# A hybrid encoder block: the first queries of group A plain behind v, returned sums as one fp32 value, a bank for each product, and queries and keys loaded over 128 partitions

## The chip, the cores and the metric

The kernel runs on one core of one Trainium2 chip. A core has five engines with instruction streams of their own: TensorE (PE) for matmuls into PSUM banks, VectorE (DVE), ScalarE (ACT) and GpSimd (POOL) for elementwise work, and SyncE (SP), which here issues nearly all transfers between DRAM and SBUF. Each engine runs its instructions in program order and waits on semaphores of the others. The metric is the device time of one execution in microseconds.

## The reference

One layer on 1024 frames of width 1024, in fp32. Eight heads (group A) attend within chunks with a learned bias, eight (group B) use stick-breaking attention; head pairs are computed together. Cut to what matters:

```
h    = rmsnorm(x, norm1_g)
proj = h @ w_in                       # q, k, v of group A, then of group B
qa, ka, va, qb, kb, vb = split(proj)
ya = chunked_attention(qa, ka, va, rel_bias)      # 64-frame chunks, 9-chunk key band, softmax
yb = stick_breaking_attention(qb, kb, vb)         # causal, 128-query blocks
mixed = concat([rmsnorm(ya, norm_a_g), rmsnorm(yb, norm_b_g)])
x = x + mixed @ w_out
x = x + conv_gated_mlp(rmsnorm(x, norm2_g), ...)  # up-projection, depthwise conv, SiLU gate, down-projection
return rmsnorm(x, final_g)
```

## The kernel before

**Precision.** Every fp32 operand of a projection is kept as two parts: a high part, rounded to the matmul type, and the low rest. A product is then three matmuls, high by high, high by low, low by high. A split is thus a copy (ScalarE or GpSimd) and a subtraction (the helper at L125, on VectorE unless said otherwise).

**Stages.** The first is the v projection by Strassen's scheme with seven products of four steps each (`steps`, in the order 1, 2, 5, 6, 7, 3, 4); between its steps a hook `extra(n)` issues work of other engines by hand. `t1` and `t2`, sums of blocks of the input's transpose, are used again later: `keep` (L367) stores their high and low parts to DRAM while v is computed, `bring_back` (L372) loads them at step (4,0), eight transfers of 512 KB, ahead of the stores of v's results by `give` (L399, and L401 for one-row stores of 2 KB each).

Then `early(n)` for n = 0 to 3 projects queries and keys of the head pairs of group B, each by seven products (`product`, L1180, twelve matmuls of 512 columns) in the order a, e, b, a, c, e, c. a and e are the two halves of one PSUM tile of two banks (`eqk`), b and c tiles of one bank. After product a, ScalarE copies a to b (L1213); after product b it copies b to c (L1234). `early_out` (L1190) scales a result, splits it and stores both parts to DRAM. `Pieces` holds the sums and splits of a pair's weights (`whole`, `make`, `split`), made one group ahead.

Then the two sweeps: four groups of group B (scores L909 and L910, scan on VectorE L918, sigmoid on ScalarE L927, transposes L945, output L959) and four of group A (scores L1009 and L1010). The text calls the head pairs B0 to B3 and A4 to A7. Between the sweeps' blocks `filler` matmuls are laid: `project_qk(n)` for n = 4 to 7 (queries and keys of group A, 48 matmuls each) and the output projection. A planner hands out filler at a rate per block (`RATE_B`, `RATES_A`) with a lead (`LEAD_B`, `LEAD_A`). `load_qk(n)` (L809) brings a pair's queries and keys: six SBUF tiles `qa, qb, ka, kb, la, lb` of 128 partitions, each filled by two transfers of 64 partitions (256 KB), high parts from `qh_d` and `kh_d`, low ones from `ql_d` and `kl_d`. The tiles are double: those of pair n+2 use the slots of pair n. Behind the sweeps come the output projection, the up- and down-projections of the channel mixer and the last norm.

Of the kernel before, what the change touches and what calls it, by code (L numbers as in the profile page):

```python
# [16 lines left out]
P = 128  # L17
T = 1024
# [39 lines left out]
def r32(ap):  # L58
    return ap.bitcast(F32)
# [3 lines left out]
def tile_hybrid_block(  # L63
# [128 lines left out]
    with tc.tile_pool(name="kp", bufs=2) as kp:  # L192
# [48 lines left out]
        def all_v():  # L241
# [104 lines left out]
                    if src is not None:  # L346
                        split(h, l, src)

            first, second = (big(f"v_x{i}") for i in range(2))
            X = area(first, second)  # L350
            steps = [(p, k) for p in (1, 2, 5, 6, 7, 3, 4) for k in range(4)]

            def staged(name):
# [2 lines left out]
                    for j in range(4)  # L356
                ]

            kept = {0: (t_high[0], t_low), 1: (t_high[1], t2_low)}
            again = {}  # L360

            def keep(n, k):
                for t, r in zip(kept[n], halves):
                    nc.sync.dma_start(t_d[n][k][:, r], r32(t[k]))

            def bring_back():
                for n in range(2):  # L367
                    for k in range(4):
                        t = slot(4 + k, f"t1_{k}", F32R) if n == 0 else kp.tile(
                            [P, T], F32R, tag=f"y{k}", name=f"t2_{k}", bufs=1  # L370
                        )
                        nc.sync.dma_start(r32(t), t_d[n][k])  # L372
                        again[n, k] = t[:, lo], t[:, hi]

            c11, u2, m5 = [], [t[:, lo] for t in xin[:4]], [t[:, hi] for t in xin[:4]]

# [26 lines left out]
            def extra(n):  # L403

                i = n - ROW_STEP
                if 0 <= i < 16:
                    S.activation(row[i % 2], row[i % 2], AF.Square, accum_out=ms[:, i : i + 1])
                    if i < 14:
                        bring_row(i + 2)
                if steps[n] == (7, 2):  # L410
                    for j in range(4):
                        S.copy(m5[j], X[j])
                    raws[0] = [wp.tile([P, D], F32, tag="wr", name="raw0_q", bufs=1)]
                    nc.sync.dma_start(raws[0][0], w_in[12])
                if steps[n] in ((5, 1), (5, 3)):
                    for k in range(n - 9, n - 7) if n == 9 else range(2, 4):
                        keep(0, k)
                if n in (12, 14):
                    for k in (0, 1) if n == 12 else (2, 3):
                        keep(1, k)  # L420
                if steps[n] == (3, 0):
                    bring_raw(0, 10)
# [12 lines left out]
                if steps[n] == (4, 1):  # L435
                    give(m5, 1, 1)
                    give(u2, 0, 1)
                if steps[n] == (4, 2):
                    ahead[0].make("s1")
                    ahead[0].split("s1")  # L440
                    ahead[0].make("s2")
                if steps[n] == (4, 3):
                    give(staged("c21"), 1, 0, Y)
                    ahead[0].split("s2")
                    bring_raw(1, 0)
                    bring_raw(2, 1)
                    bring_raw(2, 2)
                    bring_raw(3, 3)

            def t1(k):  # L450
                a = xin[k]
# [5 lines left out]
            def begin(n):  # L457
# [19 lines left out]
                if n == 7:  # L477
# [5 lines left out]
                            sums(6, k)  # L483
                    parts(6, 0)

            begin(-1)
            for n, (p, k) in enumerate(steps):
                bank = X if p in (1, 2, 5, 3) else Y
# [20 lines left out]
                "t1": [again[0, k] for k in range(4)],  # L509
                "t2": [again[1, k] for k in range(4)],  # L510
                "t3": list(zip(t_high[0], t_low)),
                "t4": list(zip(t_high[1], t4_low)),
            }

        t_d = [
            [dp.tile([P, T], F32, tag=f"t{n}{k}", name=f"t_d{n}_{k}") for k in range(4)]
            for n in range(2)
        ]
        qk_d = [
            {w: dp.tile([P, T], F32, tag=f"{w}{n}", name=f"{w}_d{n}") for w in ("qh", "ql", "kh", "kl")}  # L520
            for n in range(8)
        ]
        raws, ahead = {}, []

        def bring_raw(n, x):

# [181 lines left out]
        w_list = []  # L708
        for n in range(4, 8):
            ct = n - 4  # L710
            w_list += [(w_in[ct], f"q{n}"), (w_in[ct + 4], f"k{n}")]
# [63 lines left out]
        def spill_qk(n, what, outs, g):  # L775

            t, r = {}, rows(g)

            def high():
                t["h"] = kp.tile([P, GW], F32R, tag="tmp", name=f"{what}{n}_h{g}", bufs=3)  # L780
                (S.copy if what == "q" else GP.tensor_copy)(t["h"], t["f"])

            def keep(part, x):
                return load(256, lambda: nc.sync.dma_start(qk_d[n][f"{what}{part}"][:, r], r32(t[x])))

            head, kept = fs.pair(
                on_v(GW, lambda: scaled(outs[g], g, 0.125 if what == "q" else 1.0, f"{what}{n}", t)),
                on_s(GW, high) if what == "q" else on_g(230, high),
                keep("h", "h"),
                [on_v(GW, lambda: sub(t["f"].bitcast(F32R), t["f"], t["h"]), "VL"), keep("l", "f")],  # L790
            )
            qk_kept[n] += kept
            return head

        def load_qk(n):

            s = 6 * (n % 2)
            names = ("qa", "qb", "ka", "kb", "la", "lb")
            ts = [slot(s + i, f"{x}{n}", F32R) for i, x in enumerate(names)]
            qk_of[n] = ts  # L800
            qa, qb, ka, kb, la, lb = ts
            d = qk_d[n]
            moves = (
                ((qa, A, "qh", A), (qa, B, "ql", A), (ka, A, "kh", A), (ka, B, "kh", A), (la, A, "kl", A), (la, B, "kl", A)),
                ((qb, B, "qh", B), (qb, A, "ql", B), (kb, B, "kh", B), (kb, A, "kh", B), (lb, B, "kl", B), (lb, A, "kl", B)),
            )

            def bring(t, x, w, y):
                nc.sync.dma_start(r32(t[x, :]), d[w][y, :])  # L809

            qk_chains[n] = [
                flow.add(*(load(256, lambda m=m: bring(*m)) for m in ms), after=qk_kept[n]) for ms in moves
            ]

        def advance():

            n = len(qk_of)
            if n < 8 and at["qk"] >= n - 2 and (n < 4 or len(qk_kept[n]) == 8):
# [367 lines left out]
        def early_out(n, what, src, r, f=None):  # L1186

            if f is None:
                f = kp.tile([P, GW], F32, tag="tmp", name=f"e{what}{n}f", bufs=3)
            V.scalar_tensor_tensor(  # L1190
                out=f, in0=src, scalar=0.125 if what == "q" else 1.0, in1=rb1[:, r],
                op0=ALU.mult, op1=ALU.mult,
            )
            h = kp.tile([P, GW], F32R, tag="tmp", name=f"e{what}{n}h", bufs=3)
            S.copy(h, f)
            sub(f.bitcast(F32R), f, h)
            nc.sync.dma_start(qk_d[n][f"{what}h"][:, r], r32(h))
            nc.sync.dma_start(qk_d[n][f"{what}l"][:, r], f)

        def early(n):  # L1200

# [11 lines left out]
            S.copy(b, a)  # L1213
            if n == 0:
                ob = big("rb1_ob")
                across(ob[:, lo], rn1, 0, 4)
                across(ob[:, hi], rn1, 4, 8)
                S.copy(rb1, ob)
                for what in ("s4", "s3"):
                    own.make(what)  # L1220
                    own.split(what)
            own.split("a22")
            if n == 1:
                bring_raw(3, 10)
            if nxt:
                nxt.whole()
# [1100 lines left out]
```

## Time and profile before

| | us |
|---|---|
| median of three runs (1241.77 to 1245.99) | 1243.87 |
| profiled execution | 1245.49 |
| its span, first to last instruction | 1243.8 |
| TensorE busy in it | 1199.5 (96%) |
| v projection ends, early(0) begins | 86.5 |
| early(1) begins | 124.2 |
| early(3) ends, first filler of the sweep | 190.55 |
| first score product of the B sweep | 196.67 |
| first score product of the A sweep | 362.2 |
| first score product of pair A7 | 483.80 |

A busy row gives, for each engine, busy time, share of the span and number of instructions. Where the profile names a wait it gives the engine and line that waited, what released it, the total, the number of waits and the longest. In a table of stretches each engine has its busy time and, in brackets, its instructions; the last three columns are the granted clock, the mean busy share of the sixteen DMA engines and the GB/s that they moved.

### The profile page before, as it was taken

The page shows a single profiled execution, that of the slowest core. Times are in us where ns is not written, and L with a number is a line of the kernel's source. Part 1 is how long each engine was busy: PE and PEld are TensorE (multiplying, and loading weights), DVE is VectorE, ACT ScalarE, POOL GpSimd, SP SyncE. Part 2 cuts the span into 40 slices and gives each one's busy share as a digit, 9 for nine tenths or more (in the row PEclk, how much of TensorE's full clock was granted, in tenths as well). Part 3 has the DMA queues.
Part 4 walks back from the last instruction along what each step waited for, and adds up shares of the span by engine and source line. Part 5 has one row for each costly group of instructions (what it writes and reads, how often), then busy time and mean ns, then how long its engine had stood idle before and what let it go on. Part 6 is the DMA issues. An engine that isn't in the chain of part 4 may idle for free.

```text
span 1243.8 us, 17412 instructions
## 1 busy us (share of the span) xinstructions
PE 1199.5 (96%) x6428; PEld 992.8 (80%) x6428; DVE 944.2 (76%) x1443; ACT 688.3 (55%) x1225; POOL 153.2 (12%) x158
## 2 busy tenths in 40 slices
PE   9996898999999999989999999999999999999997
PEld 6774776888888788878878888888888888888887
DVE  7953645889857688747998776776777769969896
ACT  7772433666657677633576455555555555444424
POOL 0000012011121131044000000000000022041126
PEclk9997999999999999999999999999999999999999
DMA  8667339766865873123222212223222087330003
GB/s 291 220 202 271 119 127 269 184 177 160 211 181 165 232 220 95 52 88 124 76 102 85 96 67 92 85 68 102 76 77 102 34 325 318 128 144 1 1 1 136
DMA packets 74803, 171.14 MB, mean 138 GB/s; under 512 B 7767, under 2 KB 23255, under 8 KB 74718
## 3 DMA queue, kind: packets, MB, share of 16 engines
q1 hardware_dynamic: 74574, 169.92, 43.0%
q8 instruction: 51, 0.84, 0.3%
q14 instruction: 34, 0.28, 0.1%
q10 hardware_dynamic: 144, 0.11, 0.0%
HBM read 120.70 MB, written 49.30 MB: 137 GB/s over the span
## 4 chain that ended last, share of the span: by engine, by line
PE 66%; DVE 8%; DMA 6%; ACT 3%; issue 3%; POOL 1%; SPq 0%; DVEq 0%; ACTq 0%; POOLq 0%
PE u_a L1742 9%; PE u_c L1742 8%; PE u_e L1742 8%; PE dz L2241 8%; PE u_b L1742 4%; PE dj L2241 4%; PE dm L2241 4%; PE q_p L147 2%; PE tpb L945 2%; PE k_p L147 2%; PE yb L959 2%; PE pa L147 2%; PE dnl L2162 1%; DMA lb<-kl_d 1%; PE yy L1074 1%
## 5 line engine op out<-in xcount | busy, mean ns | idle before, releaser
L918 DVE TENSOR_TENSOR_SCAN acts<-zb,first 128x128 f32<-128x128 f32 (+7 forms) x64 | 86.4, 1351 | 15.6 <-ACT zb L927 15.6
L1766 DVE SCALAR_TENSOR_TENSOR vt<-cv,cst,vt 128x1023 f32<-128x1023 f32 (+1 forms) x44 | 58.2, 1323 | 3.3 <-ACT vt L1760 2.5
L1766 DVE SCALAR_TENSOR_TENSOR gt<-cg,cst,gt 128x1023 f32<-128x1023 f32 (+1 forms) x44 | 56.3, 1280 | 1.1 <-ACT gt L1760 0.3
L1040 ACT ACTIVATE pa<-sa,sta 128x640 f32<-128x640 f32 (+4 forms) x64 | 42.5, 665 | 18.8 <-DVE sta L1026 17.6
L927 ACT ACTIVATE zb<-zb 128x128 f32<-128x128 f32 (+7 forms) x64 | 40.9, 641 | 21.0 <-PE zb L910 19.7
L125 POOL TENSOR_TENSOR dx_0wl<-dr,dx_0wh 128x512 fp32r<-128x512 f32 x1 | 1.4, 1371 | 412.3 <-ACT dx_0wh L2008 412.3
L1760 ACT ACTIVATE gt<-cg,cst 128x1024 f32<-128x1024 f32 x22 | 27.4, 1245 | 36.9 <-DVE cg L1634 36.8
L949 ACT COPY tb<-tpb 128x128 f32<-128x128 f32 (+3 forms) x96 | 43.1, 484 | 6.4 <-PE tpb L945 5.6
L1065 ACT COPY pta<-tpa 128x512 f32<-128x512 f32 (+3 forms) x80 | 36.1, 479 | 14.6 <-PE tpa L1061 14.2
L945 PE MATMUL tpb<-ident,acts 128*128 128x128 f32 x288 | 43.2, 277 | 0.0
L1026 DVE TENSOR_REDUCE sta<-sa 128x1 f32<-128x640 f32 (+4 forms) x64 | 41.7, 654 | 1.2
L1061 PE MATMUL tpa<-ident,pa 128*128 128x128 f32 x240 | 38.3, 279 | 4.1 <-DVE sa L1022 3.1
L125 POOL TENSOR_TENSOR q_l<-q_r,q_h 128x256 fp32r<-128x256 f32 x16 | 13.3, 862 | 232.9 <-ACT q_h L740 208.9
L1631 DVE TENSOR_TENSOR up_r<-up_r 128x512 f32<-128x512 f32 x60 | 41.2, 687 | 0.8
L945 PEld LDWEIGHTS tpb<-ident,acts 128*128 128x128 f32 x288 | 33.3, 140 | 6.2 <-issue 2.6
L1061 PEld LDWEIGHTS tpa<-ident,pa 128*128 128x128 f32 x240 | 27.2, 140 | 13.1 <-ACT pta L1065 6.2
L1929 ACT COPY u_b<-u_a 128x512 f32<-128x512 f32 x19 | 10.8, 571 | 38.1 <-PE u_a L1742 38.1
L1023 DVE TENSOR_TENSOR sa<-sa,bias 128x256 f32<-128x256 f32 (+1 forms) x64 | 26.2, 413 | 6.0 <-PE sa L1010 4.8
L1074 PE MATMUL yy<-pta,v 128*64 128x128 f32 x480 | 30.0, 276 | 0.0
L959 PE MATMUL yb<-tb,dv 128*64 128x128 f32 x448 | 29.5, 273 | 0.0
L125 POOL TENSOR_TENSOR wo_l<-wo_r,wo_h 128x256 fp32r<-128x256 f32 x28 | 20.1, 745 | 70.1 <-ACT wo_h L740 70.1
L1074 PEld LDWEIGHTS yy<-pta,v 128*64 128x64 f32 x480 | 26.1, 137 | 3.3 <-issue 1.1
(1409 smaller groups left out, 4051.1 us busy)
## 6 DMA issues: line engine op xcount, KB each, us to landing
up_r<-in_w_up_dram SPq DMA_DIRECT2D x44, 512.0 KB, 3.6
act<-vt SPq DMA_DIRECT2D x22, 512.0 KB, 2.6
dr<-in_w_dn_dram SPq DMA_DIRECT2D x20, 512.0 KB, 7.0
dr<-act SPq DMA_DIRECT2D x20, 512.0 KB, 10.1
wv<-in_w_v_dram SPq DMA_DIRECT2D x16, 256.0 KB, 5.4
xin<-in_xT_dram SPq DMA_DIRECT2D x16, 256.0 KB, 5.4
row<-in_x_rows_dram SPq DMA_DIRECT2D x16, 256.0 KB, 3.2
t<-t_d SPq DMA_DIRECT2D x8, 512.0 KB, 7.7
```

Of the source, the lines that this page charges most:

```text
L147: PE.matmul(o, w[:, sl], t[:, rows(g)], start=first and i == 0, stop=last and i == 2,)
L918: V.tensor_tensor_scan(out=a[:, :w], data0=z, data1=first[:, :w], initial=1.0, op0=ALU.mult, op1=ALU.max,)
L945: PE.transpose(tp[:, cols(b)], self.a[h][:, cols(b0 + b)], ident)
L949: mine.append(flow.add(on_s(m * P, lambda o=o, tp=tp: S.copy(o, tp))))
L959: PE.matmul(yy[HS[h], :], (d if j else v)[:, off : off + 64], self.at[h][:, self.c0[h] + j * P : self.c0[h] + (j + 1) * P], start=j == 0, ...
L1026: V.tensor_reduce(out=st[:, 0:1], in_=full, axis=AX.XY if nk == 5 else AX.X, op=ALU.max, negate=True,)
L1040: on_s(w + 170, lambda: S.activation(po, full, AF.Exp, bias=st[:, 0:1], accum_out=st[:, 1:2])),
L1061: PE.transpose(tp[:, cols(b)], self.pr[src][:, cols(c)], ident)
L1074: PE.matmul(yy[HS[h], :], v[:, (i + c) * P + h * 64 : (i + c) * P + (h + 1) * 64], self.pt[:, 4 * h + c if c < 4 else 8 + h, :], start=c = ...
L1742: PE.matmul(o, w[:, cols(k)], t, start=start and k == 0 and i == 0, stop=k == 3 and i == 2, skip_group_check=True,)
L1766: V.scalar_tensor_tensor(out=t[:, : T - lag], in0=o[:, lag:], scalar=c1(c + ct), in1=t[:, : T - lag], op0=ALU.mult, op1=ALU.add,)
L2241: PE.matmul(o[m], w[:, cols(m)], t, start=i in (0, 1, 4, 5) and p == ps_[0] and j == 0, stop=p == ps_[-1] and j == 2, skip_group_check=True,)
```

## The change

It has five parts.

1. `first_query()`, called between v and early(0), computes the queries of pair 4 by the plain product (48 matmuls), with its own banks `q4_0` and `q4_1`. Their weight is loaded at step (7,2) and split at (4,0). `project_qk(4)` in the filler computes only the keys. The spreading of the norm's factor (`rb1`), `whole`, `s2`, `s4` and `s3` of the first pair move into it.
2. t1 and t2 are stored as one fp32 half each (2 MB in all in place of 4), come back behind the stores of v at step (4,2), and are split again by `split_again`: eight copies and eight subtractions.
3. The two-bank tiles of the v projection and of early(n) become tiles of one bank each (`zbank`).
4. Queries and keys are kept as `q_d[n]` and `k_d[n]` of shape `[2, P, T]` (high and low part), and a tile of 128 partitions is filled by one transfer of 512 KB: a query tile from both parts of a head, a key tile from one part, broadcast to both halves. 96 transfers become 48.
5. The rates and leads of the filler are smaller.

The core of the diff:

```diff
-RATE_B, LEAD_B = 10.0, 4.0
-RATES_A, LEAD_A = (11.0, 13.0, 13.0, 13.0), 6.5
+RATE_B, LEAD_B = 8.0, 4.0
+RATES_A, LEAD_A = (10.0, 10.0, 10.0, 10.0), 4.0
...
-            first, second = (big(f"v_x{i}") for i in range(2))
-            X = area(first, second)
+            X = [zbank(f"v_x{i}") for i in range(4)]
...
+            def keep(k):
+                nc.sync.dma_start(t_d[k], xin[k][:, hi])
+
+            def bring_back(k):
+                t = slot(k, f"t2_{k}", F32R) if k > 3 else kp.tile(
+                    [P, T], F32R, tag=f"y{k}", name=f"t1_{k}", bufs=1
+                )
+                nc.sync.dma_start(r32(t[:, hi]), t_d[k])
+                again.append(t)
+
+            def split_again(t):
+                S.copy(t[:, lo], r32(t[:, hi]))
+                sub(t[:, hi], r32(t[:, hi]), t[:, lo])
...
-                    bring_back()
-                    bring_raw(1, 11)
-                    ahead.append(Pieces(0))
-                    ahead[0].whole()
+                    lead["h"], lead["l"] = [
+                        wp.tile([P, D], F32R, tag=t, name=f"q4_{t}") for t in ("wh", "wl")
+                    ]
+                    S.copy(lead["h"], lead["r"])
+                    for r in halves:
+                        sub(lead["l"][:, r], lead["r"][:, r], lead["h"][:, r], GP)
...
                 if steps[n] == (4, 2):
+                    for k in range(KT):
+                        bring_back(k)
+                    ahead.append(Pieces(0))
                     ahead[0].make("s1")
                     ahead[0].split("s1")
-                    ahead[0].make("s2")
...
+        q_d = [dp.tile([2, P, T], F32, tag=f"q{n}", name=f"q_d{n}") for n in range(8)]
+        k_d = [dp.tile([2, P, T], F32, tag=f"k{n}", name=f"k_d{n}") for n in range(8)]
...
-            moves = (
-                ((qa, A, "qh", A), (qa, B, "ql", A), (ka, A, "kh", A), (ka, B, "kh", A), (la, A, "kl", A), (la, B, "kl", A)),
-                ((qb, B, "qh", B), (qb, A, "ql", B), (kb, B, "kh", B), (kb, A, "kh", B), (lb, B, "kl", B), (lb, A, "kl", B)),
-            )
...
+            def twice(part, h):
+                return k_d[n][part][None, h, :].to_broadcast([2, 64, T])
+
+            moves = [
+                [(q, q_d[n][:, h, :]), (k, twice(0, h)), (l, twice(1, h))]
+                for h, q, k, l in ((A, qa, ka, la), (B, qb, kb, lb))
+            ]
...
         def project_qk(n):
-            for what in ("q", "k"):
+            for what in ("q", "k") if n > 4 else ("k",):
...
-            z = big(f"eqk{n}")
-            a, e = z[:, lo], z[:, hi]
+            a, e = zbank(f"ea{n}"), zbank(f"ee{n}")
...
+        def first_query():
+
+            outs = [zbank(f"q4_{g}") for g in range(G)]
+            own = ahead[0]
+            for g in range(G):
+                for k in range(KT):
+                    mm3(outs[g : g + 1], lead["h"], lead["l"], cols(k), hh[k], hl[k], k == 0, k == KT - 1, (g,))
+                    if (g, k) == (0, 3):
+                        for i in range(2):
+                            ob = zbank(f"rb1_ob{i}")
+                            across(ob, rn1, 4 * i, 4 * i + 4)
+                            S.copy(rb1[:, rows(i)], ob)
+                    flow.work(0.68)
+                if not g:
+                    own.whole()
+                    own.make("s2")
+                    own.split("s2")
+                    again_all[0]()
+                    early_out(4, "q", outs[0], lo)
+                else:
+                    own.make("s4")
+                    own.split("s4")
+                    own.make("s3")
+                    own.split("s3")
+                    early_out(4, "q", outs[1], hi)
+
+        first_query()
```

What this makes of the order is seen at three places. The first is SyncE's queue behind early(2), where the loads of pair B0 begin. `qa` to `lb` are the SBUF tiles, the names behind the arrow the DRAM tiles, and the shape is the tile's in SBUF. Before:

```order
L809 DMA qa_1414<-qh_d_137 64x1024
L809 DMA qb_1415<-qh_d_137 64x1024
L809 DMA qa_1414<-ql_d_138 64x1024
L1197 DMA qh_d_149<-eq3h 128x512
L1198 DMA ql_d_150<-eq3f 128x512
L809 DMA qb_1415<-ql_d_138 64x1024
L809 DMA ka_1416<-kh_d_139 64x1024
L1197 DMA kh_d_151<-ek3h 128x512
L1198 DMA kl_d_152<-em_1359 128x512
L809 DMA kb_1417<-kh_d_139 64x1024
L809 DMA ka_1416<-kh_d_139 64x1024
```

and now:

```order
L803 DMA qa_1485<-q_d_137 128x1x1024
L803 DMA qb_1486<-q_d_137 128x1x1024
L1198 DMA q_d_140<-eq3h 128x512
L1199 DMA q_d_140<-eq3f 128x512
L803 DMA ka_1487<-k_d_145 128x1x1024
L1198 DMA k_d_148<-ek3h 128x512
L1199 DMA k_d_148<-em_1430 128x512
L803 DMA kb_1488<-k_d_145 128x1x1024
L1198 DMA q_d_140<-eq3h 128x512
L1199 DMA q_d_140<-eu_1431 128x512
L803 DMA la_1489<-k_d_145 128x1x1024
L803 DMA lb_1490<-k_d_145 128x1x1024
```

The twelve loads of 64 rows have become six of 128, all of them issued before the last stores of early(3)'s keys; the stores of early(3)'s queries stand behind two loads in place of three.

The second place is SyncE's queue at the end of the v projection, where t1 and t2 come back (`t`) and v is stored (`v_d`). Before:

```order
L372 DMA t_1_802<-t_d_1_134 128x1024
L372 DMA t_2_804<-t_d_2_135 128x1024
L372 DMA t_3_806<-t_d_3_136 128x1024
L529 DMA raw_11_808<-in_w_in_dram 128x1024
L399 DMA v_d_112<-xin_170 128x512
L399 DMA v_d_112<-xin_171 128x512
L399 DMA v_d_112<-xin_172 128x512
L399 DMA v_d_112<-xin_173 128x512
L399 DMA v_d_111<-xin_170 128x512
```

and now:

```order
L398 DMA v_d_111<-xin_157 128x512
L400 DMA v_d_111<-xin_157 1x512
L367 DMA t_0_821<-t_d_129 128x512
L367 DMA t_1_823<-t_d_130 128x512
L367 DMA t_2_825<-t_d_131 128x512
L367 DMA t_3_827<-t_d_132 128x512
L367 DMA t_4_829<-t_d_133 128x512
L367 DMA t_5_831<-t_d_134 128x512
L367 DMA t_6_833<-t_d_135 128x512
L367 DMA t_7_835<-t_d_136 128x512
L398 DMA v_d_112<-c_853 128x512
L398 DMA v_d_112<-c_854 128x512
```

The returns of t1 and t2 have moved behind eight stores of v and the four one-row stores, and are 512 columns wide in place of 1024.

The third is VectorE's queue around early(0). `raw` are the first pair's weights, `s_0` their sums, `t_0` to `t_7` the returned t1 and t2, `eq4f` and `eq0f` results read from PSUM banks (line 1190 before, 1191 now). Before, behind the root of the norm:

```order
L125 TENSOR_TENSOR qk0wl<-raw_q,qk0wh 128x1024
L228 TENSOR_TENSOR raw_10_705<-raw_10_705 128x512
L125 TENSOR_TENSOR s_0_859<-raw_10_705,s_0_859 128x512
L225 TENSOR_TENSOR raw_q<-raw_10_705,raw_q 128x512
L125 TENSOR_TENSOR s_0_887<-raw_q,s_0_887 128x512
L225 TENSOR_TENSOR raw_q<-raw_q 128x512
L125 TENSOR_TENSOR s_0_930<-raw_q,s_0_930 128x512
L225 TENSOR_TENSOR raw_q<-raw_q,raw_10_705 128x512
L125 TENSOR_TENSOR s_0_934<-raw_q,s_0_934 128x512
```

and now, ahead of the second bank of q4:

```order
L125 TENSOR_TENSOR qk0wl<-raw_11_683,qk0wh 128x1024
L225 TENSOR_TENSOR raw_11_683<-raw_10_685,raw_11_683 128x512
L125 TENSOR_TENSOR s_0_919<-raw_11_683,s_0_919 128x512
L125 TENSOR_TENSOR t_0_821<-t_0_821 128x512
L125 TENSOR_TENSOR t_1_823<-t_1_823 128x512
L125 TENSOR_TENSOR t_2_825<-t_2_825 128x512
L125 TENSOR_TENSOR t_3_827<-t_3_827 128x512
L125 TENSOR_TENSOR t_4_829<-t_4_829 128x512
L125 TENSOR_TENSOR t_5_831<-t_5_831 128x512
L125 TENSOR_TENSOR t_6_833<-t_6_833 128x512
L125 TENSOR_TENSOR t_7_835<-t_7_835 128x512
L1191 SCALAR_TENSOR_TENSOR eq4f<-q_0_874,rb_873 128x512
```

Eight subtractions for the returned sums stand between the first pair's `s2` and the reading of q4's first bank, a reading that was not there before; the operations of `s4` and `s3` stand behind it.

More of the change, by code (lines that the diff above doesn't have):

```diff
@@ L357, in staged @@
                 ]
[L359 to L370, printed above, removed]
-                        )
-                        nc.sync.dma_start(r32(t), t_d[n][k])
-                        again[n, k] = t[:, lo], t[:, hi]
+            again = []
+            def keep(k):
[9 more added lines that the diff above has]
+                sub(t[:, hi], r32(t[:, hi]), t[:, lo])
             c11, u2, m5 = [], [t[:, lo] for t in xin[:4]], [t[:, hi] for t in xin[:4]]
@@ L412, in extra @@
                         S.copy(m5[j], X[j])
[L413 to L420, printed above, removed]
+                    lead["r"] = wp.tile([P, D], F32, tag="wr", name="q4_r", bufs=1)
+                    nc.sync.dma_start(lead["r"], w_in[0])
+                for k in {5: (0, 1), 6: (2, 3), 7: (4, 5), 8: (6,), 9: (7,)}.get(n, ()):
+                    keep(k)
                 if steps[n] == (3, 0):
+                    bring_raw(0, 11)
                     bring_raw(0, 10)
@@ L484, in begin @@
                     parts(6, 0)
+            again_all.append(lambda: [split_again(t) for t in again])
             begin(-1)
@@ L513, in all_v, with kept_at @@
             }
[L515 to L523, printed above, removed]
+        t_d = [dp.tile([P, GW], F32, tag=f"t{k}", name=f"t_d{k}") for k in range(KT)]
+        q_d = [dp.tile([2, P, T], F32, tag=f"q{n}", name=f"q_d{n}") for n in range(8)]
+        k_d = [dp.tile([2, P, T], F32, tag=f"k{n}", name=f"k_d{n}") for n in range(8)]
+        raws, ahead, lead, again_all = {}, [], {}, []
+        def kept_at(n, what, part):
+            return {"q": q_d, "k": k_d}[what][n][part]
         def bring_raw(n, x):
@@ L783, in keep @@
             def keep(part, x):
-                return load(256, lambda: nc.sync.dma_start(qk_d[n][f"{what}{part}"][:, r], r32(t[x])))
+                return load(256, lambda: nc.sync.dma_start(kept_at(n, what, part)[:, r], r32(t[x])))
             head, kept = fs.pair(
@@ L1213, in early @@
             S.copy(b, a)
[L1214 to L1221, printed above, removed]
             own.split("a22")
             if n == 1:
+                bring_raw(3, 11)
                 bring_raw(3, 10)
```

29 lines of the change are left out of this document (13 added, 16 removed).

## The prediction

> **What bounds the kernel now.** I read the page first, then TensorE's waits up to the start of the B sweep, then the busy time by stretches, and last the transfers that the change reshapes. The page:
>
> ```profile
> span 1243.8 us, 17412 instructions
> PE 1199.5 (96%) x6428; PEld 992.8 (80%) x6428; DVE 944.2 (76%) x1443; ACT 688.3 (55%) x1225; POOL 153.2 (12%) x158
> PEclk9997999999999999999999999999999999999999
> DMA  8667339766865873123222212223222087330003
> GB/s 291 220 202 271 119 127 269 184 177 160 211 181 165 232 220 95 52 88 124 76 102 85 96 67 92 85 68 102 76 77 102 34 325 318 128 144 1 1 1 136
> DMA packets 74803, 171.14 MB, mean 138 GB/s; under 512 B 7767, under 2 KB 23255, under 8 KB 74718
> ```
>
> TensorE is busy 96% of the span, so a saving has to remove TensorE idle time or slow-clock time; the only slow slice of the clock row is the fourth, 93 to 124 us. Transfers keep the engines 0.5 to 0.8 busy while the sweeps run (slices 6 to 15), so the sweeps stay on TensorE only as long as their loads arrive. The profiled execution took 1245.49 us, 1.7 more than its span and 1.6 above the median 1243.87; the sum below is made against 1245.49.
>
> TensorE's waits between 86 and 240 us (total, number, longest):
>
> ```profile
> PE ec L1180 <- ACT ec L1234: 6.8, 1, 6.8
> PE eqk L1180 <- ACT eb L1213: 6.7, 4, 2.7
> PE zb L909 <- DVE acts L918: 3.2, 1, 3.2
> PE eb L1180 <- DMA t<-t_d: 1.8, 4, 0.7
> PE eqk L1180 <- ACT em L1230: 1.8, 1, 1.8
> ```
>
> and its timeline where early(3) ends and the sweep begins:
>
> ```profile
> 190.55 0.39 PE L147 MATMUL q_p<-hTh,q_h 128*128 128x512 f32 x1
> ...
> 196.67 0.28 PE L909 MATMUL zb<-ka,qa 128*128 128x256 f32 x1
> 200.08 0.35 PE L910 MATMUL zb<-la,qa 128*128 128x256 f32 x1 [3.13 <-DMA la<-kl_d]
> ```
>
> Between the first two stand 27 matmuls of q4: 6.12 / 27 = 0.227 us each at full clock. And the first score product already waits 3.13 us for a key load.
>
> **The change, part by part.**
>
> *The front: q4 plain behind v, fewer stored sums, a bank for each product.* The stretches of early(0), of early(1) to early(3), and of the sweep's start:
>
> ```profile
> 86.40:124.20 37.80, 26.70 (x94) 19.36 (x93) 15.20 (x23) 12.72 (x22) 0.00 (x0) 0.82 0.81 289
> 124.20:190.60 66.40, 60.45 (x254) 48.35 (x253) 36.94 (x53) 24.71 (x41) 8.41 (x11) 0.97 0.40 131
> 190.60:200.00 9.40, 6.35 (x29) 5.02 (x27) 2.68 (x4) 2.00 (x3) 0.00 (x0) 1.00 1.02 271
> ```
>
> An early group is 84 matmuls, 84 x 0.227 = 19.1 us. early(0) takes 37.8, so 18.7 are waits, slow clock and one microsecond of transposes that move elsewhere. The other three take 66.4 for 57.2, 9.2 over. The 6.8 us wait follows from the 4 MB of t1 and t2 coming back ahead of v's own stores on SyncE; now 2 MB come back, behind those stores. The four L1213 waits are product e waiting for a copy that reads the other half of its two-bank tile; with banks of their own they go, and the first e and a then wait for VectorE to read q4's banks. What stands in front of that reading on VectorE counts; the nearest rows on the chain of work are:
>
> ```profile
> 159.40 0.63 ACT eq2h L1195
> 160.05 0.70 DVE eq2f L125
> ```
>
> Ahead of the first bank's reading stand the eight new subtractions, 8 x 0.70 = 5.6 us, which cannot begin before t1 and t2 are back; ahead of the second one four more operations of `s4` and `s3` (2.8) beside the split of the first half (1.4). Over them lie q4's matmuls (48 x 0.227 = 10.9) and product a (2.7), if t1 and t2 come back in time. I bound the new waits by nothing and by 7 us (the subtractions wholly uncovered, and the split behind them) and take 5, since t1 and t2 now come back late. Gain: early(0) 18.7 - 1 - 5 = about 12; early(1) to (3) about 8; the sweep's start some 7, its 3.1 of load wait and the 3.2 for `acts` right behind it, both of which follow from early(3) ending late against the loads. Together 27; with the new waits at nothing 32, and with them at 7 and the sweep's start unchanged 18. At early(3)'s end the gain less what moved in is 12 + 8 - 10.9 - 1 = 8 us. The 48 matmuls of q4 only move: 10.9 us leave the sweeps and enter the front.
>
> *Less filler in the B sweep.* Of the 225 filler matmuls within the four B groups 186 remain, 39 x 0.227 = 8.9 us less to lay beside the scan on VectorE, which the rows of the sweep below show busy 28 to 35 of 40 us. Where VectorE is late nothing covers it: cost between 0 and 8.9, I take 4. The rates and leads only shift filler between groups; no row prices them, and the 4 holds for them too.
>
> *The loads of queries and keys.* 96 loads of 64 rows become 48 of 128. The number of bytes is the same (25.2 MB), and 48 issues on SyncE of some 0.6 us go, beside which TensorE works anyway. What changes is how a load can be cut up. The source of the new loads is `q_d[n][:, h, :]` or a key tile broadcast to `[2, 64, T]`: outermost a count of **2**, one of them with stride zero, then 64 rows of 4 KB. Before, both sides had 64 rows outermost. What the trace says of this are the seven smallest stores:
>
> ```profile
> L401 SPq DMA_DIRECT2D v_d<-xin x4: 235/236/236, 97.2 to 102.7; - x4
> L401 SPq DMA_DIRECT2D v_d<-c x2: 294/320/347, 80.5 to 81.3; - x2
> L401 SPq DMA_DIRECT2D v_d<-v_c x1: 304/304/304, 82.1 to 82.1; - x1
> ```
>
> They are single rows of 2 KB. The kernel issues 491 transfers (490 on SyncE, one on ScalarE; the view of DMA issues). If each ended with one small packet on each of 16 engines, and with the 16 rows of 128 bytes of the constants, there would be 491 x 16 + 16 = 7872 packets under 512 B. The page counts 7767, short by 105 = 7 x 15: exactly the seven stores whose outer count is 1 went over one engine, and every transfer with an outer count of 16 or more over sixteen. So the engines follow the shape. An outer count of 2 does not occur before. I take it that it gives 2 engines: no transfer of this kernel is seen cut inside its outermost count (a row of 2 KB stayed whole), and the stride between the two halves of the new source keeps them from being read as one run of 128 rows. The other reading is that the 4 KB rows inside are counted (128, so 16 engines).
>
> [...]
>
> The price, from the stretches of the sweep and the densest one of the run (last two columns: DMA share, GB/s):
>
> ```profile
> 168.00:200.00 32.00, 26.22 (x107) 20.82 (x105) 11.68 (x16) 9.65 (x15) 8.41 (x11) 0.95 0.71 203
> 200.00:240.00 40.00, 36.13 (x272) 30.41 (x273) 30.93 (x40) 22.51 (x46) 3.76 (x4) 0.96 0.86 210
> 240.00:280.00 40.00, 39.78 (x336) 33.94 (x336) 32.64 (x40) 27.15 (x52) 4.49 (x6) 1.00 0.72 191
> 280.00:320.00 40.00, 40.00 (x352) 34.56 (x349) 34.89 (x43) 26.62 (x55) 6.39 (x6) 1.00 0.70 178
> 320.00:360.00 40.00, 39.91 (x319) 33.75 (x318) 28.49 (x40) 25.01 (x49) 6.85 (x9) 1.00 0.59 170
> 360.00:400.00 40.00, 38.23 (x291) 32.40 (x291) 28.99 (x74) 29.59 (x61) 8.77 (x13) 1.00 0.69 183
> 400.00:440.00 40.00, 38.42 (x285) 32.18 (x281) 26.91 (x73) 28.45 (x67) 5.25 (x8) 1.00 0.84 248
> 440.00:480.00 40.00, 39.64 (x305) 33.53 (x304) 35.01 (x85) 28.65 (x66) 9.16 (x13) 1.00 0.65 175
> ...
> 1020.00:1030.00 10.00, 10.00 (x46) 8.24 (x44) 9.54 (x12) 4.67 (x8) 1.84 (x2) 1.00 1.03 410
> ```
>
> One busy engine moves 410 / (16 x 1.03) = 24.9 GB/s in the densest stretch, 170 / (16 x 0.59) = 18.0 in the thinnest. Half of a 524,288-byte load on each of two engines takes 262,144 B / 24.9 = **10.5 us**, up to 14.6 at 18.0. I take 10.5: the two engines would be full, as in the dense row. Over sixteen engines it is 524,288 / 410,000 = 1.3 us.
>
> These loads follow each other on the same two engines, and everything else pays its sixteenth there. From 168 to 480 us the rows move 60.7 MB; less 25.2 of these loads 35.5, of which about 2 come after the last load; 33.5 / 16 = 2.1 MB per engine, 84 us at 24.9. Where the stream begins and ends:
>
> ```profile
> L809 SPq DMA_DIRECT2D lb<-kl_d x16: 444/570/924, 192.6 to 469.3; - x16
> L809 SPq DMA_DIRECT2D qa<-qh_d x8: 445/450/1727, 175.5 to 454.5; - x8
> ...
> 483.80 0.39 PE L1009 MATMUL sa<-ka,qa 128*128 128x320 f32 x1
> ```
>
> The first load was issued at 175.5; with the front 8 us earlier it is about 167. The last head pair, A7, began its scores at 483.80, so 1245.5 - 483.8 = 762 us of work lie behind that point. Six loads of a head pair take 6 x 10.5 = 63 us, and with the other traffic 63 + 84 / 8 = 74, against (483.8 - 200) / 7 = 41 us of computing per pair. Slots are double: the loads of pair n+2 wait only for pair n, so the stream never runs dry and it sets the pace. A7 cannot begin before 47 loads and the other traffic are through: 167 + 47 x 10.5 + 84 = **744 us**, and the end is 744 + 762 = **1506**, say 1505. The front's 27 us are lost in it: TensorE only waits longer for B's first pair (6 loads behind 167: 230 us, against 200 before).
>
> **Rivals.** *All sixteen engines share these loads* (a cut by 4 KB rows). Then the loads cost what they cost before, the front's gain stays, and the time is 1245.5 - 27 + 4 = **1223**. For it: the missing 105 packets fit this reading too, since the seven stores are single rows. Against: the cut would have to be made across two dimensions, which nothing in this trace shows. This is the case on the other side; it decides from where six loads and 84 / 8 = 10.5 us of other traffic fit into a pair's 41 us, that is 5.1 us a load; four engines (21 / 4 = 5.3) are just short of it.
>
> *The same, and the B sweep falls to VectorE*: the whole 8.9 us of cover is lost, and the new waits on q4's banks take their upper bound (2 more): 1245.5 - 25 + 9 = **1230**. For it: 34.89 of 40 us busy in 280 to 320; against: in 320 to 400 a quarter is free.
>
> *Two engines, and bubbles in the stream.* The weights and the stores of k4 to k7 stand on SyncE among the loads and on the same two engines, and TensorE meets their matmuls in program order. Where a weight lands behind a pair's backlog (63 us), the pair's slots come free late, and the two engines run dry. If each of the eight pairs loses one load's length, 10.5 us, that is 1505 + 84 = **1589**. For it: SyncE issues in order; against: 74 - 41 = 33 us of slack per pair.
>
> **How the numbers follow.** Two engines, steady stream: 0.68 (own range 1400 to 1560: at the low end the other traffic is not in the way, 167 + 494 + 762 = 1423, and the engines are some 5% quicker than the densest row; at the high end 11.4 us a load and as much more for the rest). Two engines with bubbles 0.16 (1560 to 1640). Sixteen engines 0.12; sixteen with VectorE in the way 0.04. The first two hold 0.84, so the range is 1400 to 1640, and the sixteen-engine cases lie outside it. A measurement of this kernel can tell some 0.3% from no change; faster by more than that: 0.15 (both sixteen-engine cases but a sliver), within it 0.01, slower 0.84.
>
> **What would show it.** Two engines: from issue to landing a query or key load takes tens of microseconds in place of 5 to 8; from 170 to about 740 us TensorE is busy little more than half, its waits naming `qa`, `ka` or `la` loads; the DMA row shows 0.2 to 0.3 there at some 100 GB/s; A7 starts near 744; behind it the stages are as long as before; 56 transfers are gone, so packets under 512 B fall to 7767 - 56 x 16 = 6871, and with two engines to 6871 - 48 x 14 = 6199. Front: no wait of `ec` on L1234's copy, q4's 48 matmuls ahead of early(0), early(0) ending at about 124 with q4 done. I am wrong if the loads land within 10 us: then the time is near 1223, and the shape rule that I read from single-row stores does not hold for a count of 2.

## The result and the profile after

| | before | after |
|---|---|---|
| median, us | 1244.74 (4 runs) | 1587.53 (4 runs) |
| ratio, 95% interval | 1 | 1.2755 [1.2728, 1.2782] |
| profiled execution, us | 1245.49 | 1587.85 |
| early(3) ends | 190.55 | 182.21 |
| first score product of A7 | 483.80 | 806.93 |
| from there to the end of the execution | 762 | 781 |

The kernel is 27.6% slower, and 323 of the 342 us between the two profiled executions are lost before A7. The page after, with the rows that were shown of before:

```profile
span 1586.0 us, 17350 instructions
PE 1222.8 (77%) x6428; PEld 1013.1 (64%) x6428; DVE 948.0 (60%) x1451; ACT 693.9 (44%) x1234; POOL 152.4 (10%) x156
PEclk9999957776768695967869999999999999999998
DMA  7463222213131312225221231222222222933003
GB/s 270 155 249 140 108 97 98 75 53 101 63 101 64 100 75 97 84 92 172 73 81 41 90 136 67 93 82 91 81 88 85 81 80 94 399 111 140 1 1 107
DMA packets 72211, 166.94 MB, mean 105 GB/s; under 512 B 6199, under 2 KB 21687, under 8 KB 72126
```

TensorE does the same 6428 matmuls, but they fill 77% of the span. In the sweeps (slices 5 to 20) the transfers move 91 GB/s on average, about half of the 193 of before (slices 6 to 15 there), while the mean busy share of the sixteen engines is 0.1 to 0.3 in all slices but one: most engines are idle. The packets under 512 B are 6199, the number worked out for two engines per wide load; sixteen would give 6871. SyncE's timeline in the middle of the B sweep (start, duration), and the VectorE operation that waits for its last line:

```profile
309.22 11.71 SPq L803 DMA_DIRECT2D ka<-k_d  x1
320.98 9.77 SPq L803 DMA_DIRECT2D kb<-k_d  x1
330.80 9.78 SPq L803 DMA_DIRECT2D la<-k_d  x1
340.62 9.78 SPq L803 DMA_DIRECT2D lb<-k_d  x1
350.51 9.71 SPq L872 DMA_DIRECT2D dv<-v_d  x1
360.32 10.30 SPq L873 DMA_DIRECT2D v<-v_d  x1
370.71 9.15 SPq L1357 DMA_DIRECT2D spill<-yb  x4
...
378.77 0.75 DVE L1351 SCALAR_TENSOR_TENSOR yb<-y,cst,yb 128x512 fp32r<-128x512 f32 x1 [48.07 <-DMA spill<-yb]
```

The first two wide loads, at 171.5 and 172.15 us, took SyncE 0.6 and 0.5 us to issue. Here, with earlier ones still under way, each issue takes as long as a load, and the loads follow each other 9.8 us apart: 262,144 B / 9.8 us = 26.7 GB/s on each of two engines. From 309.2 to 360.3 us the sixteen engines are 0.13 busy in the mean, at 53 GB/s in all; two of sixteen are 0.125.

TensorE's waits over the whole kernel, the longest nine groups (total, number, longest):

```profile
PE zb L910 <- DVE acts L919: 144.1, 5, 46.6
PE tpa L1062 <- DVE rn L1099: 46.4, 1, 46.4
PE tpa L1062 <- ACT pa L1034: 46.0, 1, 46.0
PE zb L911 <- DMA la<-k_d: 38.5, 2, 21.8
PE zb L910 <- DMA ka<-k_d: 20.3, 1, 20.3
PE sa L1010 <- ACT pa L1041: 18.0, 1, 18.0
PE zb L911 <- DMA lb<-k_d: 11.4, 2, 6.1
PE sa L1011 <- DMA la<-k_d: 8.1, 1, 8.1
PE sa L1011 <- DMA lb<-k_d: 7.1, 1, 7.1
```

They add up to 340 us. Only 85 of them name a query or key load. The others name VectorE or ScalarE, so the next view is what VectorE waits for between 160 and 840 us:

```profile
DVE yb L1351 <- DMA spill<-yb: 136.5, 4, 48.1
DVE acts L919 <- ACT zb L928: 64.5, 21, 21.4
DVE k_f L765 <- DMA q_d<-q_f: 48.5, 1, 48.5
DVE bias L971 <- DMA bias<-in_toep_dram: 46.2, 1, 46.2
DVE sa L1023 <- PE sa L1011: 25.5, 12, 9.4
DVE x L1151 <- DMA x<-in_xT_dram: 19.8, 1, 19.8
```

From about 331 us on VectorE stands still once per pair, for 20 to 48 us, until a store out of a buffer that it wants again (`spill<-yb`, `q_d<-q_f`: three buffers of one kind serve them all), or a load of bias or x, has landed. By the packet count these are transfers over sixteen engines, but they stand behind the next pair's wide loads on SyncE's queue: ScalarE had written the data of the store at 370.71 by 321.5 us, but in SyncE's order it comes behind six wide loads (four of them above) and two loads of v, and VectorE goes on 8 us after it was issued. The scan, the scores and TensorE wait behind VectorE.

### The profile page after: what moved, and what is told of

Same layout as the page of the kernel before. It is cut to its first block, busy times and chain, and to the rows that moved or that the text cites. A ratio compares the mean times of both kernels' runs of the same rounds, so it can differ in the third digit from the quotient of the medians.

```text
span 1586.0 us, 17350 instructions
## 1 busy us (share of the span) xinstructions
PE 1222.8 (77%) x6428; PEld 1013.1 (64%) x6428; DVE 948.0 (60%) x1451; ACT 693.9 (44%) x1234; POOL 152.4 (10%) x156
## 2 busy tenths in 40 slices
DMA packets 72211, 166.94 MB, mean 105 GB/s; under 512 B 6199, under 2 KB 21687, under 8 KB 72126
## 4 chain that ended last, share of the span: by engine, by line
PE 58%; SPq 19%; DMA 14%; DVE 5%; ACT 2%; issue 1%; POOL 0%; DVEq 0%; ACTq 0%; POOLq 0%
SPq L803 12%; PE u_a L1762 7%; PE u_c L1762 7%; PE u_e L1762 7%; PE dz L2261 6%; DMA lb<-k_d 4%; PE u_b L1762 3%; PE dj L2261 3%; PE dm L2261 3%; PE v_x L493 3%; PE pa L147 2%; DMA spill<-yb 2%; DMA la<-k_d 2%; PE v_y L493 2%; DMA bias<-in_toep_dram 2%; DMA q_d<-q_f 2%
## 5 line engine op out<-in xcount | busy, mean ns | idle before, releaser
L910 PE MATMUL zb<-kb,qb 128*128 128x512 f32 (+3 forms) x48 | 20.1, 419 | 144.1 <-DVE acts L919 144.1
L1062 PE MATMUL tpa<-ident,pa 128*128 128x128 f32 x240 | 42.0, 298 | 96.1 <-DVE rn L1099 46.4
L910 PEld LDWEIGHTS zb<-kb,qb 128*128 128x128 f32 x48 | 10.3, 215 | 146.9 <-DVE acts L919 146.0
L1351 DVE SCALAR_TENSOR_TENSOR yb<-y,cst,yb 128x512 fp32r<-128x512 f32 x8 | 6.0, 750 | 141.2 <-DMA spill<-yb 136.5
L946 PE MATMUL tpb<-ident,acts 128*128 128x128 f32 x288 | 47.1, 294 | 0.0
L911 PE MATMUL zb<-la,qa 128*128 128x512 f32 (+3 forms) x48 | 17.0, 360 | 38.5 <-DMA la<-k_d 38.5
L765 DVE SCALAR_TENSOR_TENSOR k_f<-k_p,rb 128x512 f32<-128x512 f32 x8 | 5.5, 687 | 53.9 <-DMA q_d<-q_f 48.5
L911 PEld LDWEIGHTS zb<-la,qa 128*128 128x128 f32 x48 | 9.6, 199 | 40.4 <-DMA la<-k_d 39.0
L910 PE MATMUL zb<-ka,qa 128*128 128x512 f32 (+3 forms) x48 | 18.1, 379 | 20.3 <-DMA ka<-k_d 20.3
```

Of the source, the lines that this page charges most:

```text
L910: PE.matmul(z[:, o : o + n], q[:, cols(i)], k[:, ks], start=True, stop=False)
L946: PE.transpose(tp[:, cols(b)], self.a[h][:, cols(b0 + b)], ident)
L1062: PE.transpose(tp[:, cols(b)], self.pr[src][:, cols(c)], ident)
```

## The experiments

**The loads by halves.** The changed kernel, with each tile filled by two transfers of 64 rows.

```diff
...
-                [(q, q_d[n][:, h, :]), (k, twice(0, h)), (l, twice(1, h))]
+                [(q, y, q_d[n][i, h, :]) for i, y in enumerate((A, B))]
+                + [(t, y, k_d[n][i, h, :]) for i, t in enumerate((k, l)) for y in (A, B)]
...
```

> The changed kernel, with each query and key tile filled again by two transfers of 64 partitions (256 KB, 64 rows outermost on both sides); all else as changed. If the whole loss is the outer count of 2, the sweeps run as before and the front's gain shows: 1215 to 1235 us, first score product of A7 near 460 us, and packets under 512 B at 6199 + 48 x 14 + 48 x 16 = 7639. If the front, the banks or the thinner filler carry part of the loss, it stays above 1300 us.

Measured: 1228.1 us, ratio to before 0.9877 [0.985, 0.9904]. The packet row of its page, and four rows of its TensorE timeline:

```profile
DMA packets 73651, 166.95 MB, mean 136 GB/s; under 512 B 7639, under 2 KB 23127, under 8 KB 73566
...
182.00 0.39 PE L147 MATMUL k_p<-hTh,k_h 128*128 128x512 f32 x1
...
188.12 0.28 PE L912 MATMUL zb<-ka,qa 128*128 128x256 f32 x1
192.69 0.58 PE L913 MATMUL zb<-la,qa 128*128 128x256 f32 x1 [4.30 <-DMA la<-k_d]
...
466.17 0.39 PE L1012 MATMUL sa<-ka,qa 128*128 128x320 f32 x1
```

The whole loss is in the shape of these loads; without it the rest of the change makes the kernel faster. The packet count is the forecast one. early(3) ends 8.5 us earlier than before, A7 begins 17.6 earlier (466.2 us, where 460 was expected); the wait for `la` at the sweep's start is still there (4.30 us against 3.13).

**The wide loads alone.** The kernel before, with nothing but `q_d`, `k_d` and the 48 loads of the change.

> The kernel before, with nothing changed but the queries' and keys' DRAM tiles and their 48 loads over 128 partitions with an outer count of 2. If that count alone does it: 1570 to 1620 us, loads issued 9.7 us apart where they follow each other, and packets under 512 B at 7767 - 48 x 16 - 48 x 14 = 6327. If other parts of the change are needed for the loss, it comes out below 1400 us.

Measured: 1586.2 us, one run, with this packet row:

```profile
DMA packets 73363, 171.14 MB, mean 108 GB/s; under 512 B 6327, under 2 KB 21815, under 8 KB 73278
```

So the loads alone give the whole loss, to within 2 us of the full change, and the front's gain is lost in it.

**Wide, with an outer count of 128.** Still 48 loads of 512 KB over 128 partitions, but out of DRAM tiles whose 128 rows lie in a row. The stores that fill them are split by head, and each key part is stored twice.

```diff
...
-        k_d = [dp.tile([2, P, T], F32, tag=f"k{n}", name=f"k_d{n}") for n in range(8)]
+        k_d = [
+            [[dp.tile([P, T], F32, tag=f"k{n}{h}{i}", name=f"k_d{n}{h}{i}") for i in range(2)] for h in range(2)]
+            for n in range(8)
+        ]
...
-                [(q, q_d[n][:, h, :]), (k, twice(0, h)), (l, twice(1, h))]
+                [(q, q_d[n][h]), (k, k_d[n][h][0]), (l, k_d[n][h][1])]
...
```

> The changed kernel, still with 48 loads of 512 KB over 128 partitions, but from DRAM tiles of 128 rows in a row (each query and key store is split by head, and a key part is stored twice, 8.4 MB more written), so that the outer count is 128. If the outer count is the cause, it runs on sixteen engines: 1220 to 1250 us. If loads of 512 KB over 128 partitions are slow by themselves, it stays near 1580 us.

> The kernel with 48 loads of 512 KB over 128 partitions whose outer count is 128, timed in rounds. 1223 to 1231 us: the same as with loads by halves (1228.1), since SyncE's issues and the 8.4 MB of second key stores lie beside other work; ratio to the kernel before 0.985 to 0.990. If 48 fewer loads were worth anything of their own it would be under 1223.

Measured: 1226.7 us in one run, and 1225.3 us as the median of four, ratio 0.987 [0.9847, 0.9893]. So neither the size of the load nor its 128 partitions make the loss; the outer count of the source does. This form and the one by halves beat both kernels and can't be told apart by their intervals. That 48 loads fewer are worth anything by themselves is not shown.

**Queries alone, keys alone.** Sixteen or 32 wide loads in place of 48, the others by halves.

> The changed kernel, with only the queries loaded over 128 partitions with an outer count of 2 (16 such loads), the keys by halves of 64 rows. If the two engines bind only where their queue is longer than a pair's work, 2 x 9.8 + 16 us of other traffic per pair lie under 41 us of work, and the time is 1220 to 1260 us. If any load on two engines holds up the stores and loads behind it in full, a third of the loss stays: 1223 + 365 / 3 = 1345 us.

> The changed kernel with only the keys loaded over 128 partitions with an outer count of 2 (32 such loads), the queries by halves. If every such load costs the pair its time in full, as with 16 (130 us, 8.1 each) and 48 (360 us, 7.5 each): 1228 + 32 x 7.8 = 1478 us, taken as 1450 to 1500. If only the stream beyond a pair's 41 us of work costs: 4 x 9.75 + 10.5 = 49.5 us per pair, 1228 + 8 x 8.5 = 1296 us.

Measured: 1358.2 and 1466.5 us, one run each. From 1228.1 without any, a wide load costs 130.1 / 16 = 8.1, 238.4 / 32 = 7.5 and, in the full change, 359.4 / 48 = 7.5 us, of the 9.8 that it occupies. Two queries take 19.6 us per pair, which with other traffic is below the 41 us of a pair's work, and yet they are paid nearly in full. So there the loss isn't the part of the stream that work fails to cover. With queries alone, VectorE's timeline has a shorter stop about once per pair; three of them:

```profile
281.64 0.75 DVE L1353 SCALAR_TENSOR_TENSOR yb<-y,cst,yb 128x512 fp32r<-128x512 f32 x1 [10.63 <-DMA q_d<-q_h]
344.42 0.75 DVE L1353 SCALAR_TENSOR_TENSOR yb<-y,cst,yb 128x512 fp32r<-128x512 f32 x1 [16.31 <-DMA spill<-yb]
396.80 0.75 DVE L1353 SCALAR_TENSOR_TENSOR yb<-y,cst,yb 128x512 fp32r<-128x512 f32 x1 [12.67 <-DMA k_d<-k_h]
```

They are 3 to 9 us shorter than two loads, as those of 42 to 48 us in the full change are 1 to 7 us shorter than five.

**The stores on another queue.** If VectorE's waits for stores hold the pairs up, they must go when the stores leave SyncE's queue. Tried from ScalarE's queue with all loads wide and with queries wide, then from GpSimd's.

```diff
-                return load(256, lambda: nc.sync.dma_start(kept_at(n, what, part)[:, r], r32(t[x])))
+                return load(256, lambda: nc.scalar.dma_start(kept_at(n, what, part)[:, r], r32(t[x])))
...
-                    return load(256, lambda: nc.sync.dma_start(spill[n][i][:, r], r32(t[i])))
+                    return load(256, lambda: nc.scalar.dma_start(spill[n][i][:, r], r32(t[i])))
```

> The changed kernel with its 48 wide loads, but the sweeps' stores of queries, keys and of group B's outputs are issued from ScalarE's queue in place of SyncE's. If what makes the pairs lose more than the stream of loads is that VectorE waits for buffers whose stores stand behind the loads on SyncE's queue, its four waits for such stores (48.1, 41.6, 45.4 and 48.5 us) go and the stream of loads binds: A7 near 171.5 + 47 x 9.75 + 84 = 714, the end near 714 + 781 = 1495, taken as 1440 to 1520 us. If the two engines hold up every transfer alike, from whatever queue, the waits stay and the time is 1570 to 1600 us.

> The kernel with only the queries wide (1358.2 us), with the same stores issued from ScalarE's queue. If stores behind the loads cause the 15 us that each pair loses there, about five of the eight waits go (those for bias and x loads stay): 1265 to 1300 us. If it is the engines' backlog whatever the queue: 1345 to 1365 us.

Measured: 1550.4 us, between the two expectations, and 1359.7 us, no gain. With queries wide, ScalarE's timeline shows why (ACTq are its issues); the last row is of the view of line 783, where these stores are issued:

```profile
242.76 0.33 ACTq L783 DMA_DIRECT2D k_d<-k_h  x1
243.20 0.90 ACT L930 ACTIVATE zb<-zb 128x896 f32<-128x896 f32 x1 [24.03 <-DMA qb<-q_d]
...
L783 ACTq EVENT_SEMAPHORE  x19: 17/17/17, 242.7 to 562.2; - x19
```

The sigmoid at 243.20 does not read `qb`; the issue of a store stands directly ahead of it, and by the profile ScalarE was held there until a wide load had landed. What stands there is a semaphore instruction of ScalarE's own at that line, the first of 19 at 242.7 us, and so a wait that the program carries. The stop has moved from VectorE to ScalarE, so this pair of runs could not decide.

> The changed kernel with its 48 wide loads, the same stores as in the run with ScalarE now issued from GpSimd's queue. There ScalarE waited at each issue until an earlier wide load had landed. If GpSimd's issues do not wait for SyncE's loads, VectorE's waits for stores (48.1, 41.6, 45.4, 48.5 us) go, and the stream of loads binds: 1440 to 1520 us. If its issues or its transfers wait for the loads as well: 1540 to 1600 us.

> The kernel with only the queries wide (1358.2 us; 1359.7 with these stores on ScalarE's queue), the stores issued from GpSimd's queue. If the stores no longer wait for the loads, the five of eight waits that came from them go: 1265 to 1300 us. If they wait all the same: 1340 to 1365 us.

Measured: 1548.2 and 1333.4 us, 39 and 25 us less than with these stores on SyncE. The first is within the range for waiting all the same, but not for that reason; the second lies between its two ranges. VectorE's longest waits in the first, and its stores of group B's outputs with the median time from issue to landing, are:

```profile
DVE bias L971 <- DMA bias<-in_toep_dram: 117.5, 3, 46.9
DVE acts L919 <- ACT zb L928: 76.7, 23, 27.8
DVE dv L877 <- DMA v<-v_d: 75.4, 2, 44.4
...
spill<-yb POOLq DMA_DIRECT2D x16, 256.0 KB, 5.9
```

The stores land a median of 5.9 us after their issue, though the wide loads pass on two engines each as before (6199 packets under 512 B here too); in the kernel before, from SyncE and with the loads by halves, the one such landing that the profile gives took 5.9 as well. So it was their place in SyncE's order that held the stores up, and not that the two engines were busy. They are gone from the top, and loads of v and bias, still behind the wide loads on SyncE, stop VectorE just as long. One more run sends these from GpSimd too:

```diff
...
-                nc.sync.dma_start(o, src[:P])
-                nc.sync.dma_start(nxt, src[1:])
+                nc.gpsimd.dma_start(o, src[:P])
+                nc.gpsimd.dma_start(nxt, src[1:])
...
-                load(256, lambda: nc.sync.dma_start(bias, toep[:, 2 * p : 2 * p + 2, :])),
+                load(256, lambda: nc.gpsimd.dma_start(bias, toep[:, 2 * p : 2 * p + 2, :])),
```

> As the run with stores on GpSimd's queue (1548.2 us), and the loads of v and of the bias issued there too, for which VectorE waited in their place (44.4, 31.0, 42.0, 28.6 and 46.9 us). If waiting transfers of this kind are the whole of what the pairs lose beyond the stream of wide loads, that stream binds now: near 714 + 781 = 1495, taken as 1440 to 1515 us. If each pair finds a further transfer behind the loads (weights of the filler, x), or the slots of the loads themselves bind: 1520 to 1560 us.

Measured: 1530.9 us, in the second range. Now SyncE's timeline runs without a gap from one pair's loads into the next in the B sweep, and TensorE waits for the loads themselves (its waits for `ka`, `la` and `lb` add up to 165 us, against 85 in the full change). After 565 us two further stops name weights of the filler that are still on SyncE's queue (ScalarE's timeline); at the end of the second one TensorE also waits, 33 us, for `yh<-spill`, a load in the same queue:

```profile
349.88 9.75 SPq L803 DMA_DIRECT2D lb<-k_d  x1
359.73 9.71 SPq L803 DMA_DIRECT2D qa<-q_d  x1
369.55 9.72 SPq L803 DMA_DIRECT2D qb<-q_d  x1
...
593.87 1.04 ACT L739 CAST k_h<-k_r 128x1024 fp32r<-128x1024 f32 x1 [46.59 <-DMA k_r<-in_w_in_dram]
684.73 1.05 ACT L739 CAST wo_h<-wo_r 128x1024 fp32r<-128x1024 f32 x1 [31.86 <-DMA wo_r<-in_w_out_dram]
```

From 171.1 to 512.1 us its pairs follow each other every 341 / 5 = 68 us, against (566.3 - 171.5) / 5 = 79 in the full change. That is the stream which the prediction had reckoned at 74: six loads of 9.8 are 59 us of it, and 9 are left for the rest, where 10.5 were reckoned. More of the three shared buffers, the direct test, wasn't tried.

**The old rates of the filler**, with the loads by halves.

```diff
-RATE_B, LEAD_B = 8.0, 4.0
-RATES_A, LEAD_A = (10.0, 10.0, 10.0, 10.0), 4.0
+RATE_B, LEAD_B = 10.0, 4.0
+RATES_A, LEAD_A = (11.0, 13.0, 13.0, 13.0), 6.5
```

> The kernel with loads by halves (1228.1 us) with the rates and leads of the filler as they were before the change. If the thinner filler of the B sweep gives back some of the front's gain (4 us reckoned): 1222 to 1227 us. If VectorE does not miss the cover, or the rates do nothing: 1226 to 1231 us.

Measured: 1235.7 us, ratio 0.995 [0.993, 0.9971], against 0.9877 [0.985, 0.9904] with the new ones. Both expectations missed it: the new rates are worth some 8 us, about half of what the change gains with the loads by halves. By which wait was not followed up.

## Why the prediction was right, and where not

**The cause was right.** Two engines carry each wide load, read from a source with an outer count of 2: the packet counts show the two, and the wide loads alone, the same loads by halves and those with an outer count of 128 show that this makes the loss. The reading by 4 KB rows is out. The packets under 512 B agree with one engine at an outer count of 1 (7767 before, where sixteen for every transfer would give 7872), two at 2 (6199), and sixteen at 64 (7639 with the loads by halves) and at 128 (8919 with that outer count, which has 128 more stores: 6871 + 128 x 16). That the loads follow each other on the same two engines, which the stream rests on, no view of before shows; after, they come 9.8 us apart with the sixteen engines 0.13 busy, as if on one pair, and no view names the engines.

**The likeliest case was not the one that came.** 1505 rested on the step "the loads of pair n+2 wait only for pair n, so the stream never runs dry and it sets the pace". What failed is the tacit half of it, that pair n computes in 41 us while pair n+1's loads pass. Pair n needs stores, bias and v that stand behind those loads, so it stops until they are through, and only then makes room for pair n+2. The terms: first load at 171.5 in place of 167; a load 9.8 us, not 10.5, so 47 of them 461 and not 494; with the 84 of other traffic, which no run measures by itself, A7 would have begun at 716. It began at 807, so 91 us are left, and gaps in the stream are the reading of them that the stops above support. Behind A7 stand 781 in place of 762 us, 15 of the 19 in A7's own waits for `la` and `lb`. (The DMA row of before reads 0.3 to 0.9 in slices 6 to 15, not 0.5 to 0.8; no term rests on it.)

**The rival with bubbles is what happened**, put at 1589 with a chance of 0.16, against 1587.5. The mechanism was named, transfers on SyncE's queue among the loads, but the wrong ones in front: it had weights land late, and it was stores and bias that stopped the pairs, and the weights only once these had been taken away. It also counted on the two engines being shared; the stores from GpSimd, which share them too and land after a median of 5.9 us, show that SyncE's order was what held stores up. Its price, one load's length per pair, was an assumption, and that the sum agrees is in part luck: the loads took 33 us less than reckoned, and the later start (4.5), the gaps (91 against 84) and the longer work behind A7 (19) made up for it.

**The point from which it decides was wrong.** The 5.1 us a load, below which the two engines were to be hidden, went with the same step. Queries alone, 19.6 us per pair, cost 130 us.

**The rival with sixteen engines** was put at 1223; the kernel with halves takes 1228.1, with an outer count of 128 1225.3. With the halves early(3) ended 8.5 us earlier where 8 were reckoned. The 6.8 us wait of `ec` is gone; 4.5 us of a new wait came, near the 5 allowed, but for ScalarE's copy ahead of early(0)'s product b and not for VectorE's reading of q4's banks. By the start of the A sweep the two kernels had done the same 1999 matmuls, and it came 15.2 us earlier (347.0 against 362.2) where 27 - 4 = 23 were reckoned: of the 7 us at the sweep's start the 3.1 of load wait did not go, 4.30 stand in their place, and the rest was not followed up. The 4 us of cost that were to hold for the rates as well had the wrong sign for these: the new rates gain some 8 us.

## What to carry to other kernels

Before merging transfers, write down the outermost count of the source: here a leading 2, from a part index (the queries, 130 us) or a broadcast (the keys, 238 us), left a load two of sixteen engines, and a layout whose 128 rows lie in a row (1225.3 us), or two transfers (1228.1 us), avoided it. Don't count such a load as hidden because the work beside it is longer: here what stood behind it on SyncE's queue, stores out of scarce buffers above all, kept VectorE waiting up to 48 us, and 7.5 to 8.1 of a load's 9.8 us were paid. Where the waits of an engine name another engine, follow them until a transfer is named, and when one such wait has been removed look for the next transfer in the same queue: here bias (117.5 us) and v (75.4) took the place of the stores.

## What the runs showed of the hardware

Where wide loads follow each other, an issue on SyncE takes as long as a load, 9.8 us in place of the 0.6 of before, so what stood later in SyncE's order moved with it: the store of 370.71 us, whose data were written by 321.5. The same stores, issued from GpSimd beside these loads, landed after a median of 5.9 us; behind them on SyncE's queue VectorE waited up to 48 us for one. And the same 6428 matmuls are busy 1222.8 us in place of 1199.5, the mean granted clock being 0.883 in place of 0.990: but for the last slice, the clock row falls below 0.9 only within slices 6 to 21, the stretch in which TensorE waits.
